# Gate and up of a SwiGLU as a two by two block product with seven multiplications, half of the tokens at a time

## The chip, the cores and the metric

The kernel runs on one core of a Trainium2 chip. The metric is the device time in microseconds (us). The core has a matrix engine (TensorE, PE in the rows), a vector engine (VectorE, DVE), an activation engine (ScalarE, ACT), a general engine (GpSimd, POOL), and queues that start transfers; weights stream from DRAM, and sums of matmuls build up in PSUM. Each engine takes its own instructions in their order.

## What is computed

The reference is one layer of a decoder on 1032 tokens (1024 of a prompt, 8 samples), with D = 1024 features and an inner width of 2816 in both feed-forward parts:

```
def swiglu(x, wg, wu, wd):
    return (silu(x @ wg) * (x @ wu)) @ wd

h = x + 1/2 * swiglu(rms(x), wg1, wu1, wd1)      # first feed-forward part
z = rms(h) @ w_in                                # input projection
h = h + concat(rms(attention(z)), headrms(mlstm(z))) @ w_out
h = h + 1/2 * swiglu(rms(h), wg2, wu2, wd2)      # second feed-forward part
y = rms(h + sigmoid(rms(h) @ w_ple_gate) * (p @ w_ple_proj))
```

All of it is float32. The kernel splits each float32 operand into a rounded part `hi` and a rest `lo`, and makes each product of two tiles from three matmuls (hi hi, hi lo, lo hi).

## The kernel before

Features lie on the partitions, tokens along the free axis. The tokens are cut in G = 3 groups of N = 344. `loadw` loads a weight tile and `split` makes its two parts: a cast on ScalarE (L178) and a subtraction on VectorE (L182), on GpSimd where it is told so (L180).

In a feed-forward part (`ffn`) a unit is one tile of 128 inner features and one token group: `mmg` makes 24 matmuls of 128x344 for gate into PSUM tile `pg`, 24 for up into `pu` (L196 to L198), then ScalarE takes silu, VectorE multiplies (L353) and splits the product into `hdh` and `hdl`. Each of the 22 inner tiles has its gate and up weights loaded and split once, for all three groups. After a block of inner tiles (`FBLOCKS` = 5, 5, 5, 5, 2) the down product follows: for each of 8 output tiles and each group one PSUM tile `pd`, added to the residual stream `h` by VectorE (L365).

At the start (`begin`) the first part multiplies x by the norm's gain alone (`lift`, L293) and leaves each token's scale to what follows the products (L347, L349), so that TensorE starts before the sums of squares are known. Elsewhere the norms of the next part (`norm_a`, `norm_b`; L249 to L279) are made group by group, while TensorE still works on the other groups: in the last block of an `ffn` (`halves`, `close`), and in the input projection behind it.

The order on each engine is that of the program text as `Emitter` hands it out; tiles in SBUF come from one ring (`big`, 43 tiles), PSUM has 8 tiles.

## Time and profile before

| | us |
|---|---|
| median of 3 runs | 2420.05 |
| lowest, highest run | 2419.57, 2423.83 |
| span of the profiled execution | 2381.1 |
| around the span (median less span) | 38.95 |
| TensorE busy | 2294.8 |
| VectorE busy | 1084.0 |
| ScalarE busy | 732.8 |
| GpSimd busy | 416.5 |

The span runs from the first to the last instruction of the profiled execution. A run's time is longer than that by what lies ahead of the first and behind the last instruction. A matmul's duration in the rows reaches from its entry to the end of its result, and matmuls overlap; what one costs in a stream is the distance from one start to the next.

### The profile page before, as it was taken

Reading aid. Unit: us, or ns where it says so; the run is one execution under the profiler, and the core shown is the slowest. Engines: PE = TensorE matmul, PEld = TensorE weight load, DVE = VectorE, ACT = ScalarE, POOL = GpSimd, SP = SyncE. Lnnn points to the kernel's source line nnn. Section 1 sums busy time; section 2 is a strip of 40 time slices with the busy share of each in tenths; the row PEclk is TensorE's granted clock in tenths of the full one; section 3 lists DMA queues with packets and bytes.
Section 4 is the critical chain, followed back from the end, with each engine's and each line's share of the span. In section 5 each row is a group of like instructions: output and inputs, shape, how many; then the busy total and the mean of one; then the engine's idle time right before and its main releaser. Section 6 shows DMA issues by size and latency. Waiting matters only on the chain.

```text
span 2381.1 us, 35330 instructions
## 1 busy us (share of the span) xinstructions
PE 2294.8 (96%) x14479; PEld 2220.7 (93%) x14479; DVE 1084.0 (46%) x2231; ACT 732.8 (31%) x1496; POOL 416.5 (17%) x403
## 2 busy tenths in 40 slices
PE   8999999999998999999888889999999999999997
PEld 7999999999998999999666679999999999999996
DVE  7332332333335656447766677623223223223575
ACT  5211211202213334444655553411121120211353
POOL 4101101101103321102565314200000000000233
PEclk9999999999999999999989989999999999999998
DMA  3111011120121313224964530111111112112213
GB/s 134 38 52 60 29 55 54 32 75 28 43 75 59 109 48 93 82 86 165 260 164 134 160 136 28 45 38 52 55 33 54 56 32 70 33 38 78 62 38 107
DMA packets 77883, 177.84 MB, mean 75 GB/s; under 512 B 11200, under 2 KB 37408, under 8 KB 77720
## 3 DMA queue, kind: packets, MB, share of 16 engines
q1 hardware_dynamic: 67432, 153.22, 21.1%
q0 software_dynamic: 6832, 18.12, 2.9%
q10 hardware_dynamic: 3456, 4.23, 0.6%
q8 instruction: 114, 1.87, 0.3%
q14 instruction: 49, 0.40, 0.1%
HBM read 146.58 MB, written 28.95 MB: 74 GB/s over the span
## 4 chain that ended last, share of the span: by engine, by line
PE 82%; DVE 9%; DMA 4%; ACT 3%; issue 2%; POOL 1%; SPq 0%; ACTq 0%; DVEq 0%; POOLq 0%
PE pd L197 7%; PE pd L198 7%; PE pd L196 7%; PE pg L198 7%; PE pu L197 7%; PE pu L196 7%; PE pu L198 7%; PE pg L197 7%; PE pg L196 7%; PE pz L197 3%; PE pz L196 3%; PE pz L198 3%; DVE xf L279 2%; PE po L1211 1%; DMA kt<-in_cT,idx_t 1%
## 5 line engine op out<-in xcount | busy, mean ns | idle before, releaser
L196 PE MATMUL pd<-hdh,wh 128*128 128x344 f32 x1056 | 341.0, 323 | 5.8 <-ACT hdh L178 5.8
L197 PE MATMUL pd<-hdl,wh 128*128 128x344 f32 x1056 | 340.0, 322 | 3.4 <-DVE hdl L182 3.3
L197 PE MATMUL pg<-xn,wh 128*128 128x344 f32 x1056 | 338.6, 321 | 4.5 <-DVE xn L182 3.8
L198 PE MATMUL pd<-hdh,wl 128*128 128x344 f32 x1056 | 339.7, 322 | 0.0
L196 PE MATMUL pg<-xn,wh 128*128 128x344 f32 x1056 | 338.1, 320 | 0.9 <-ACT xn L178 0.9
L196 PE MATMUL pu<-xn,wh 128*128 128x344 f32 x1056 | 338.5, 321 | 0.3 <-DVE si L347 0.3
L198 PE MATMUL pu<-xn,wl 128*128 128x344 f32 x1056 | 337.8, 320 | 0.8 <-DVE wl L182 0.8
L198 PE MATMUL pg<-xn,wl 128*128 128x344 f32 x1056 | 337.9, 320 | 0.5 <-DVE wl L182 0.3
L197 PE MATMUL pu<-xn,wh 128*128 128x344 f32 x1056 | 337.9, 320 | 0.0
L178 ACT CAST wh<-wr 128x1024 fp32r<-128x1024 f32 (+2 forms) x195 | 180.4, 935 | 371.8 <-PE pd L197 291.2
L182 DVE TENSOR_TENSOR wl<-wr,wh 128x1024 fp32r<-128x1024 f32 (+2 forms) x195 | 215.5, 1105 | 116.3 <-ACT wh L178 111.5
L353 DVE TENSOR_TENSOR hp<-si,pu 128x344 f32<-128x344 f32 x132 | 67.7, 513 | 420.5 <-PE pu L198 413.0
L365 DVE SCALAR_TENSOR_TENSOR h<-pd,h 128x344 f32<-128x344 f32 x240 | 123.2, 515 | 280.1 <-PE pd L198 280.1
L254 POOL TENSOR_TENSOR sq<-sq,sq 128x344 f32<-128x344 f32 x66 | 70.6, 1070 | 798.6 <-ACT sq L249 770.7
L196 PEld LDWEIGHTS pd<-hdh,wh 128*128 128x128 f32 x1056 | 200.0, 189 | 7.1 <-ACT hdh L178 6.7
L197 PEld LDWEIGHTS pg<-xn,wh 128*128 128x128 f32 x1056 | 198.7, 188 | 6.4 <-DVE xn L182 5.2
L197 PEld LDWEIGHTS pd<-hdl,wh 128*128 128x128 f32 x1056 | 200.0, 189 | 4.6 <-DVE hdl L182 4.2
L198 PEld LDWEIGHTS pd<-hdh,wl 128*128 128x128 f32 x1056 | 200.0, 189 | 0.0
L196 PEld LDWEIGHTS pg<-xn,wh 128*128 128x128 f32 x1056 | 198.6, 188 | 1.5 <-ACT xn L178 1.2
L198 PEld LDWEIGHTS pg<-xn,wl 128*128 128x128 f32 x1056 | 198.7, 188 | 1.1 <-DVE wl L182 1.1
L198 PEld LDWEIGHTS pu<-xn,wl 128*128 128x128 f32 x1056 | 198.6, 188 | 1.1 <-DVE wl L182 1.1
L196 PEld LDWEIGHTS pu<-xn,wh 128*128 128x128 f32 x1056 | 198.6, 188 | 1.0 <-issue 0.8
(384 smaller groups left out, 4174.9 us busy)
## 6 DMA issues: line engine op xcount, KB each, us to landing
wr<-in_wu SPq DMA_DIRECT2D x44, 512.0 KB, 3.6
wr<-in_wg SPq DMA_DIRECT2D x43, 512.0 KB, 3.7
wr<-in_wd SPq DMA_DIRECT2D x64, 320.0 KB, 2.9
wr<-in_w_in SPq DMA_DIRECT2D x22, 512.0 KB, 3.8
h<-in_xT SPq DMA_DIRECT2D x24, 172.0 KB, 4.2
hsp<-h SPq DMA_DIRECT2D x8, 516.0 KB, 3.4
ppd<-pj SPq DMA_DIRECT2D x24, 172.0 KB, 2.2
h<-hsp SPq DMA_DIRECT2D x8, 516.0 KB, 5.9
```

What stands on the lines that cost most here:

```text
L178: act.copy(hi, src)
L182: dve.tensor_tensor(out=lo, in0=src, in1=hi.bitcast(F32), op=ALU.subtract)
L196: pe.matmul(ps, whi, xhi, start=first, stop=False)
L197: pe.matmul(ps, whi, xlo, start=False, stop=False)
L198: pe.matmul(ps, wlo, xhi, start=False, stop=last)
L254: pool.tensor_tensor(out=acc[0], in0=acc[0], in1=q, op=ALU.add)
L279: dve.scalar_tensor_tensor(out=x, in0=s[:, c], scalar=gc[:, g0 + k:g0 + k + 1], in1=r, op0=ALU.mult, op1=ALU.mult)
L353: dve.tensor_tensor(out=p, in0=s, in1=pu, op=ALU.mult)
L365: dve.scalar_tensor_tensor(out=h[m][:, c], in0=pd, scalar=0.5, in1=h[m][:, c], op0=ALU.mult, op1=ALU.add)
L1211: pe.matmul(po[:, j0 * 128:512], vtok[kb][:, hd, :], px[:, i, j0:4, :].rearrange("p j q -> p (j q)"), start=(kb == 0 and i == 0), stop=(kb ...
```

## The change

The tokens are cut in four quarters of 258 instead of three groups of 344, in the whole kernel. A feed-forward part goes through all its 22 inner tiles for one half of the tokens (two quarters), then through all of them again for the other half. Gate and up are taken as chains: a chain is two inner tiles, one of the two matrices, one half of the tokens. Its weights are four blocks (two inner tiles by two halves of the 1024 features, a11 to a22), its tokens four blocks (two halves of the features by two quarters), and the product of the two by two blocks is made from seven block products of 4 x 3 matmuls of 128x258, 84 in all, where eight would be the plain way. There are 22 chains per half.

The token operands `b11, b21, t2, t1, t3, t4, b22` are made once per half in `operands` (16 multiplications of 128x258, four differences of 128x1032, seven splits of 128x1032). The weight operands are made per chain in `weights`: three splits of 128x1024, one of 128x512, two sums of 128x512 on GpSimd and two on VectorE. As the weights are used by one half and then by the other, they are loaded, combined and split twice. The results are put together from PSUM: ScalarE copies three partial sums per chain (c1, u2, u3), VectorE adds three. The down products (blocks of 4 and at last 2 inner tiles) are put between the block products (`pump`). The norm of the first half is made before the chains begin (there is no `lift`), that of the second half at the end of the first half's chains. `h` is kept as two halves, one of which goes to DRAM and back.

```diff
-G = 3
+G = 4
 N = T // G
...
-FBLOCKS = [5, 5, 5, 5, 2]
+PBLOCKS = [2, 2, 2, 2, 2, 1]
+NP = NF // 2
+NCH = 2 * NP
+HC = T // 2
+HALF = ((0, 1), (2, 3))
...
+    NAMES = ("b11", "b21", "t2", "t1", "t3", "t4", "b22")
+
+    def operands(h, hf, rs, g0, x):
+        def put(n, src):
+            hi, lo = B([128, 4, N], F32R, "xh"), B([128, 4, N], F32R, "xl")
+            split(hi, lo, src)
+            x[n] = (hi, lo)
...
+        b11 = block(0, 0)
+        put("b11", b11)
+        yield
+        b21 = block(1, 0)
+        put("b21", b21)
+        yield
+        b12 = block(0, 1)
+        t1 = comb(b12, b11)
+        b11 = None
+        b22 = block(1, 1)
+        t2 = comb(b22, t1)
+        put("t2", t2)
+        yield
+        put("t1", t1)
...
+        comb(b22, b12, b12)
+        put("t3", b12)
...
+        comb(b21, t2, b21)
+        put("t4", b21)
...
+        put("b22", b22)
+
+    def weights(ap, j):
+        r1, r2 = (B([128, 2, 512], F32, "wr") for _ in range(2))
...
+            put(("b11", "b21"), r1)
+            s1 = B([128, 512], F32, "ws")
+            pool.tensor_tensor(out=s1, in0=a21, in1=a22, op=ALU.add)
+            pool.tensor_tensor(out=a21, in0=a11, in1=a21, op=ALU.subtract)
+            dve.tensor_tensor(out=a11, in0=s1, in1=a11, op=ALU.subtract)
+            yield
+            dve.tensor_tensor(out=a12, in0=a12, in1=a11, op=ALU.subtract)
+            put(("t2", "b22"), r1)
+            yield
+            hl = B([128, 2, 512], F32R, "wa")
+            split(hl[:, 0], hl[:, 1], s1)
+            o["t1"] = (hl[:, 0], hl[:, 1])
+            yield
+            put(("t3", "t4"), r2)
...
+        def start(i):
+            c = st[i] = {"b1": PS([128, N], "c1"), "b2": PS([128, N], "c2"), "b3": None}
...
+            product(c["b1"], i, "b11", True)
+            c["c1"] = SC(p="c1")
+            act.copy(c["c1"], c["b1"])
+            product(c["b2"], i, "b21", True)
+            dve.tensor_tensor(out=c["o"][:, 0], in0=c["b2"], in1=c["c1"], op=ALU.add)
...
+        def u2(i):
+            c = st[i]
+            product(c["b1"], i, "t2", False)
+            c["u2"] = SC(p="u2")
+            act.copy(c["u2"], c["b1"])
+            c["b3"] = PS([128, N], "c3")
+            product(c["b3"], i, "t1", True)
...
+        ready(0)
+        want(1)
+        for i in range(NCH):
+            start(i)
+            if i:
+                c21(i - 1)
+            want(i + 2)
+            ready(i + 1, 1)
+            u2(i)
+            ready(i + 1, 1)
+            if i:
+                c12(i - 1)
+            ready(i + 1, 1)
+            u3(i)
+            ready(i + 1)
+            after_chain(i)
...
+        ffn_half(h, 0, x, wg, wu, wd, pre, chain_a, tail_a)
+        drain(box["g"])
+        after(0)
+        ffn_half(h, 1, x2, wg, wu, wd, pre2, lambda i: last(i - NCH), last)
+        after(1)
```

In the rows that follow a name's number tells tiles apart; `xf` and `xt` are token blocks, `xl` and `wl` the rests of split token and weight operands.

VectorE at the program's start, before: from its third instruction on it lifts the slices of x as they land and splits the first weight tile behind two of them.

```order
L293 TENSOR_SCALAR xf_131<-h_79,gc 128x344
L293 TENSOR_SCALAR xf_135<-h_80,gc 128x344
L182 TENSOR_TENSOR xn_93<-xf_135,xn_92 128x344
L182 TENSOR_TENSOR wl_141<-wr_139,wh_140 128x512 x2
L293 TENSOR_SCALAR xf_154<-h_81,gc 128x344
L293 TENSOR_SCALAR xf_158<-h_82,gc 128x344
L293 TENSOR_SCALAR xf_162<-h_83,gc 128x344
L293 TENSOR_SCALAR xf_166<-h_84,gc 128x344
```

After: the last of its rows ahead of, and up to, the first chain's weights (`wl_245` is the rest of `b11, b21`; 27 rows for sums of squares, norms and blocks stand ahead of these).

```order
L334 SCALAR_TENSOR_TENSOR xf_215<-h_115,gc,rk_148 128x258 x2
L339 TENSOR_TENSOR xt_220<-xf_215,xt_213 128x1032
L339 TENSOR_TENSOR xf_208<-xf_215,xf_208 128x1032
L339 TENSOR_TENSOR xf_199<-xf_199,xt_220 128x1032
L183 TENSOR_TENSOR xl_223<-xt_220,xh_222 128x1032
L183 TENSOR_TENSOR xl_227<-xt_213,xh_226 128x1032
L183 TENSOR_TENSOR xl_232<-xf_208,xh_231 128x1032
L183 TENSOR_TENSOR xl_237<-xf_199,xh_236 128x1032
L183 TENSOR_TENSOR xl_241<-xf_215,xh_240 128x1032
L183 TENSOR_TENSOR wl_245<-wr_120,wh_244 128x1024
L389 TENSOR_TENSOR wr_120<-ws_248,wr_120 128x512
L391 TENSOR_TENSOR wr_120<-wr_120 128x512
```

The first weight rest moved from the fourth of these rows, ahead of most of the tokens, to a place behind all of the token operands.

VectorE in the middle of the first feed-forward part, before, where a block's down products are added to the residual and the next weights are split:

```order
L365 SCALAR_TENSOR_TENSOR h_79<-pd_4086,h_79 128x344
L365 SCALAR_TENSOR_TENSOR h_79<-pd_4103,h_79 128x344
L365 SCALAR_TENSOR_TENSOR h_79<-pd_4120,h_79 128x344
L182 TENSOR_TENSOR wl_4310<-wr_4308,wh_4309 128x640
L365 SCALAR_TENSOR_TENSOR h_80<-pd_4143,h_80 128x344
L365 SCALAR_TENSOR_TENSOR h_80<-pd_4160,h_80 128x344
L365 SCALAR_TENSOR_TENSOR h_80<-pd_4177,h_80 128x344
L182 TENSOR_TENSOR wl_4367<-wr_4365,wh_4366 128x640
L365 SCALAR_TENSOR_TENSOR h_81<-pd_4200,h_81 128x344
L365 SCALAR_TENSOR_TENSOR h_81<-pd_4217,h_81 128x344
```

After, at the change from the first to the second half of the tokens (`xl_4388` to `xl_4450` and `xt` are operands of the second half, `pd_4477` a down product of the first, `wl_4412` the rest of the weights of the first half's last eight down products):

```order
L466 SCALAR_TENSOR_TENSOR h_113<-pd_4477,h_113 128x258
L466 SCALAR_TENSOR_TENSOR h_113<-pd_4485,h_113 128x258
L339 TENSOR_TENSOR xt_4378<-xf_4373,xf_4327 128x1032
L334 SCALAR_TENSOR_TENSOR xf_4380<-h_3714,gc,rk_3928 128x258 x2
L334 SCALAR_TENSOR_TENSOR xf_4380<-h_3715,gc,rk_3928 128x258 x2
L339 TENSOR_TENSOR xt_4385<-xf_4380,xt_4378 128x1032
L339 TENSOR_TENSOR xf_4373<-xf_4380,xf_4373 128x1032
L339 TENSOR_TENSOR xf_4350<-xf_4350,xt_4385 128x1032
L183 TENSOR_TENSOR xl_4388<-xt_4385,xh_4387 128x1032
L183 TENSOR_TENSOR xl_4406<-xt_4378,xh_4405 128x1032
L183 TENSOR_TENSOR wl_4412<-wr_4409,wh_4411 128x1024
L183 TENSOR_TENSOR xl_4425<-xf_4373,xh_4424 128x1032
```

The weights of the last down products came to stand behind the operands of the second half.

VectorE in the middle of the units, before: scale of a unit's gate, product with up, splits.

```order
L347 TENSOR_TENSOR si_3262<-pg_3212,qz 128x344
L182 TENSOR_TENSOR wl_3330<-wr_3328,wh_3329 128x1024
L353 TENSOR_TENSOR hp_3266<-si_3262,pu_3213 128x344
L182 TENSOR_TENSOR wl_3336<-wr_3334,wh_3335 128x1024
L182 TENSOR_TENSOR hdl_3153<-hp_3266,hdh_3152 128x344
L347 TENSOR_TENSOR si_3320<-pg_3270,qz 128x344
L353 TENSOR_TENSOR hp_3324<-si_3320,pu_3271 128x344
L182 TENSOR_TENSOR hdl_3153<-hp_3324,hdh_3152 128x344
```

After, in the middle of the chains (`wr_1869` and `ws_2076` are weight blocks being combined, `wl_2129` and `wl_2179` rests of weight operands, `hp` and `gs` results):

```order
L389 TENSOR_TENSOR wr_1869<-ws_2076,wr_1869 128x512
L527 TENSOR_TENSOR hp_1993<-c_317_2094,u_326_2175 128x258
L391 TENSOR_TENSOR wr_1869<-wr_1869 128x512
L543 TENSOR_TENSOR hp_1993<-hp_1993,gs_1799 128x258
L466 SCALAR_TENSOR_TENSOR h_114<-pd_2197,h_114 128x258
L183 TENSOR_TENSOR wl_2110<-wr_2107,wh_2109 128x1024
L511 TENSOR_TENSOR hp_1993<-c_302_1991,gs_1799 128x258
L183 TENSOR_TENSOR wl_2129<-wr_1869,wh_2128 128x1024
L466 SCALAR_TENSOR_TENSOR h_114<-pd_2239,h_114 128x258
L183 TENSOR_TENSOR wa_2160<-ws_2076,wa_2160 128x512
L183 TENSOR_TENSOR wl_2179<-wr_1870,wh_2178 128x1024
L500 TENSOR_TENSOR gs_2184<-c_330_2183,c_333_2211 128x258
```

Where before one or two whole weight splits stood between the rows that read PSUM, there are now two sums and four splits per chain (`wl_2110` belongs to a down product).

## Rows read from the trace of the kernel before

**Rows 1.** The page: span, busy time of each engine, shares of the chain that ended last.
```profile
span 2381.1 us, 35330 instructions
...
PE 2294.8 (96%) x14479; PEld 2220.7 (93%) x14479; DVE 1084.0 (46%) x2231; ACT 732.8 (31%) x1496; POOL 416.5 (17%) x403
...
PE 82%; DVE 9%; DMA 4%; ACT 3%; issue 2%; POOL 1%; SPq 0%; ACTq 0%; DVEq 0%; POOLq 0%
```

**Rows 2.** Windows (start:end, length; busy us and instructions per engine; clock, DMA, GB/s).
```profile
0.00:20.00 20.00, 16.13 (x87) 14.52 (x88) 15.22 (x29) 11.81 (x26) 8.06 (x12) 1.00 0.91 315
20.00:150.00 130.00, 124.54 (x775) 121.58 (x775) 64.39 (x102) 43.26 (x79) 31.15 (x30) 1.00 0.13 41
150.00:300.00 150.00, 150.00 (x954) 150.00 (x953) 45.66 (x75) 26.18 (x43) 14.28 (x14) 1.00 0.15 47
...
750.00:800.00 50.00, 41.89 (x243) 40.05 (x243) 43.62 (x66) 23.04 (x45) 22.52 (x20) 0.93 0.40 142
...
2220.00:2300.00 80.00, 75.47 (x456) 73.18 (x455) 58.10 (x87) 40.66 (x75) 30.17 (x27) 0.98 0.19 56
```

**Rows 3.** Timeline of TensorE: the warming-up (start, duration in us, count).
```profile
1.07 5.56 PE L443 MATMUL pw<-ones 128*128 128x128 f32 x28 [1.07 <-DVE epsc L426]
```

**Rows 4.** Matmul groups by form (count, busy us, mean ns, idle time before).
```profile
L196 PE MATMUL pd<-hdh,wh 128*128 128x344 f32 x1056 | 341.0, 323 | 5.8 <-ACT hdh L178 5.8
...
L197 PE MATMUL pg<-xn,wh 128*128 128x344 f32 x1056 | 338.6, 321 | 4.5 <-DVE xn L182 3.8 <-POOL xn L180 0.8
...
L197 PE MATMUL pj<-pel,wj 128*128 128x344 f32 x48 | 16.9, 351 | 0.0
```

**Rows 5.** Timeline of TensorE: 256 columns, then 512.
```profile
1156.22 0.28 PE L1164 MATMUL pss<-kTh,qTh 96*128 96x256 f32 x1
1156.34 0.28 PE L1165 MATMUL pss<-kTl,qTh 96*128 96x256 f32 x1
1156.45 0.28 PE L1166 MATMUL pss<-kTh,qTl 96*128 96x256 f32 x1
1156.57 0.39 PE L196 MATMUL ps<-uvh,ckh 128*128 128x512 f32 x1
1156.80 0.40 PE L197 MATMUL ps<-uvh,ckh 128*128 128x512 f32 x1
```

**Rows 6.** Timeline of TensorE: sixteen matmuls of one column and the next one.
```profile
943.26 1.84 PE L806 MATMUL pb<-sq,ct 128*128 128x1 f32 x16
944.96 0.40 PE L196 MATMUL pz<-u,wh 128*128 128x344 f32 x1
```

**Rows 7.** VectorE groups by form, whole span.
```profile
L182 DVE TENSOR_TENSOR wl<-wr,wh 128x1024 fp32r<-128x1024 f32 x129 | 160.4, 1244 | 79.9 <-ACT wh L178 79.7
L365 DVE SCALAR_TENSOR_TENSOR h<-pd,h 128x344 f32<-128x344 f32 x240 | 123.2, 515 | 280.1 <-PE pd L198 280.1
...
L182 DVE TENSOR_TENSOR PT<-pT,PT 128x512 fp32r<-128x512 f32 x48 | 32.2, 684 | 6.0 <-ACT PT L178 5.6
...
L279 DVE SCALAR_TENSOR_TENSOR z<-z,gc,r 128x344 f32<-128x344 f32 x15 | 7.7, 570 | 0.0
```

**Rows 8.** ScalarE groups by form, whole span.
```profile
L178 ACT CAST wh<-wr 128x1024 fp32r<-128x1024 f32 x129 | 132.7, 1043 | 128.7 <-PE pd L197 111.3 <-DMA wr<-in_wd 5.4 <-DMA wr<-in_wu 4.9
...
L267 ACT ACT_TABLE_LOAD x10 | 12.8, 1283 | 31.7 <-PE ns L263 31.6
```

**Rows 9.** Timelines: one VectorE operation twice, and GpSimd beside the second.
```profile
763.10 0.52 DVE L182 TENSOR_TENSOR hdl<-hp,hdh 128x344 fp32r<-128x344 f32 x1
...
768.21 1.22 DVE L182 TENSOR_TENSOR hdl<-hp,hdh 128x344 fp32r<-128x344 f32 x1
...
766.00 4.20 POOL L254 TENSOR_TENSOR sq<-sq,sq 128x344 f32<-128x344 f32 x4
```

**Rows 10.** GpSimd groups by form, whole span.
```profile
L349 POOL TENSOR_TENSOR si<-si,mask_qk 128x344 f32<-128x344 f32 x22 | 20.4, 926 | 364.2 <-ACT si L348 364.2
...
L799 POOL TENSOR_TENSOR vb<-vb,kws 128x1024 f32<-128x1024 f32 x4 | 7.6, 1899 | 65.4 <-DMA vb<-vsd 42.6 <-DVE nst L796 22.7
```

More of the change, by code (lines that the diff above doesn't have):

```diff
@@ L426, in trunk @@
     dve.memset(epsc, EPS)
[L427 to L433 removed]
+    h = Rows()
     warm = C([128, 1], name="warm")
@@ L484, in consts, with ffn, chain_a, tail_a @@
             sp.dma_start(out=t, in_=I[n])
[L485 to L489 removed]
+        dve.memset(qzr, 0.0)
+    def ffn(g0, wg, wu, wd, first_rows, first_scales, next_rows, after, last, x=None):
+        pre = ({}, {}, {})
+        if x is None:
+            x = {}
+            first_rows()
+            pre[0][0] = weights(wg, 0)
+            drain(operands(h, 0, first_scales(), g0, x))
+        box = {}
+        def chain_a(i):
+            if i == NCH - 3:
+                next_rows()
+            if i == NCH - 2:
+                box["s"] = [stat(h, g) for g in HALF[1]]
+            if i == NCH - 1:
+                box["r"] = [s() for s in box.pop("s")]
+        pre2 = ({}, {}, {})
+        x2 = {}
+        def tail_a(n):
+            if n == 0:
+                pre2[0][0] = weights(wg, 0)
+                box["g"] = operands(h, 1, box.pop("r"), g0, x2)
+            next(box["g"], None)
+        ffn_half(h, 0, x, wg, wu, wd, pre, chain_a, tail_a)
[3 more added lines that the diff above has]
+        after(1)
@@ new lines, in rows_x, with scales_x, following, apply @@
+    def rows_x():
+        act.activation(warm, epsc, RSQ)
+        pw = PS([128, 128], "pw")
+        for i in range(WARM):
+            pe.matmul(pw, ones, ones, start=i == 0, stop=i == WARM - 1)
+        sp.dma_start(out=gc, in_=I["gcols"])
+        h.load(I["xT"], 0)
+    def scales_x():
+        fs = [stat(h, g) for g in HALF[0]]
+        return [f() for f in fs]
+    def following(x, g0, keep, ahead):
+        scales = {}
+        def apply(g):
+            x.alloc(g)
+            scaled(scales[g // 2][g % 2], h.srcs(g), x.outs(g), g0)
+        def after(hf):
+            box = []
+            def sums():
+                box.extend(stat(h, g) for g in HALF[hf])
+            def rest():
+                scales[hf] = [f() for f in box]
+                if hf == 0:
+                    h.spill(hsp, 0)
+                else:
+                    apply(2)
+                    apply(3)
+                    if not keep:
+                        h.spill(hsp, 1)
+            if hf == 0:
+                em.later(3.0, sums)
+                em.later(9.0, rest)
+            else:
+                sums()
+                em.later(5.0, rest)
+        def last(n):
+            if n == -2:
+                h.load(hsp, 0)
+            if n == 1:
+                apply(0)
+            if n == 6:
+                apply(1)
+                if not keep:
+                    h.t[0] = None
+                ahead()
+        return after, last
```

521 lines of the change are left out of this document (278 added, 243 removed).

## The prediction

> **What bounds the kernel now.** The first look is at the page [rows 1]: TensorE is busy for 2294.8 of 2381.1 us, and 82% of the chain that ended last is TensorE's; VectorE is busy for 46%. So the kernel is bound by its stream of matmuls, and an edit counts by the matmuls that it takes out and by the holes that it puts in. Next come windows, since a share over the whole span hides where the holes are [rows 2]. From 150 to 300 us, in the units of the first feed-forward part, TensorE never stops: 954 matmuls in 150 us, or 157.2 ns for one of 128x344. By that price the other windows show their holes. From 0 to 150 us there are 862 instructions, 28 of them the warming-up [rows 3], so 834 matmuls of 157.2 ns = 131.1 us, and 18.9 us are lost at the start. From 750 to 800 us (end of the first part, start of the input projection) 243 x 157.2 ns = 38.2 us, so 11.8 us are lost. From 2220 to 2300 us (end of the second part) 456 x 157.2 ns = 71.7 us, so 8.3 us are lost. VectorE works 45.66 us of the 150, 30%: inside the units it has room.
>
> **The sum's base.** The profiled execution has a span of 2381.1 us. The median is 2420.05, so 38.95 us lie around the span; I leave these as they are and add the span's change to the median.
>
> **Term 1, the seven products.** There are 6 groups of 1056 gate and up matmuls, 6336 [rows 4]; by 157.2 ns they cost 996 us. After the change there are 4 halves (two parts, two halves each) x 22 chains x 84 = 7392 of 128x258. The trace has none of 258 columns. The nearest rows are three of 256 columns: starts 1156.22, .34, .45 and 1156.57, so 0.35 / 3 = 117 ns; the 512 behind them takes 0.23 us [rows 5]. So the price is proportional to the columns: 117 x 258/256 = 117.9, and 157.2 x 258/344 = 117.9. A floor lies close below: sixteen matmuls of one column take 1.70 us, 106 ns each [rows 6], which is the weight load alone. I take 117.9: 7392 x 117.9 = 871.5 us, a gain of **124.5 us**. All other matmuls of 344 (down to the 3 x 48 of `pj`, 6264 in all [rows 4]) become 4/3 as many at 3/4 of the price: 8352 x 117.9 = 984.7 = 6264 x 157.2, nothing. That zero and the gain hang on the same price: a nanosecond more for each of the 15744 is 16 us. Bounds: 117 ns (-14 us) and 122 ns, if the small excess of [rows 5] were larger in this stream (+64 us).
>
> A rule of the Trainium skill speaks against this term. TensorE: Matmul & The Clock Gate, section Back-to-back issue gap, says that a stream of weight load and matmul pairs is spaced by both, and gives about 81 ns at 128 columns and 131 ns at 512, which is mostly a fixed cost; on that line 258 columns would cost about 0.9 of 344 instead of 0.75 (an estimate from that page). Then 7392 x 0.9 is 6650 against 6336, and the change would lose in its main term and in all the rest. Here [rows 2, 5] give 117, 157.2 and 230, which is a line through nearly zero; the measurement decides, and what is left of the rule is rival 3.
>
> **Term 2, the start.** Before, the first matmul needs one lifted slice and half a weight tile. After, VectorE has 37 rows up to `wl_245`, without which the first product is not complete. Their prices: a subtraction of 128x1024 takes 1.24 us, of 128x512 0.68, a sum of 344 from PSUM 0.515, a scalar_tensor_tensor of 344 from SBUF 0.57 [rows 7]; on the line through these, 258 columns cost 0.41 (0.48 for the last kind). Six sums and eight steps of the norm at 0.41, sixteen multiplications at 0.48, eleven differences and splits of 1032 and one of 1024 at 1.24: 5.7 + 7.7 + 14.9 = 28.3 us. Half of x is 2.1 MB, at 315 GB/s [rows 2] 6.7 us, landed at about 9; behind it the squares end, and the norm's ScalarE step with its table load of 1.28 us [rows 8] stands in the chain, so the norm's steps begin at about 13.5 us, with some 26 us of VectorE to come. The first product starts at about 39.5 us. The combined weights behind it (5.8 us of VectorE against two products of 1.4 us) hold it for one or two us more, and TensorE comes in cold. I take 41 us lost instead of 18.9: **+22 us** (16 to 27).
>
> **Term 3, the middle of each part, new and twice.** When the first half's last chain ends with its product b22, TensorE has 4 down products of 12 and 8 of 6 matmuls left that it can do, 96 x 117.9 ns = 11.3 us, then 8 that need `wl_4412`. VectorE has, from the sum behind b22 to `wl_4412`: 16 multiplications (7.7), nine differences and splits of 1024 or 1032 (11.2), three rows of 516 (2.1), 13 of 258 from PSUM (0.41, as the 0.515 of 344 [rows 7]; 5.3): 26.3 us. TensorE waits 15 us. The 48 matmuls then last 5.7 us, as long as VectorE's next rows, but the combined weights of the next chain (two sums, three splits) come a few us late: 3 us. Coming out of such a hole has a price too: around the 4.8 us of waits in the window of 750 to 800 us the granted clock is 0.93 [rows 2], 3.5 us of 50 lost; as part of that is in the waits I take 2. Together 20 us each, **+40 us** (28 to 54). What is late there is nothing but VectorE's queue; ScalarE's casts (1.04 us [rows 8]) run ahead of it.
>
> **Term 4, the other ends.** At the end of the first part, the quarters of the first half have their norm done long before, and eight units of the input projection (22.6 us) can run while the last two quarters' norm is made: the 11.8 us mostly vanish, **-10**. At the end of the second part the per-layer weights' splits stand behind the norm's rows: 18.5 us of VectorE, some 2.5 us of latencies, less 5.9 us of matmuls in hand, so 16 to 18 us instead of 8.3: **+9**. The second part's first operands are made beside the last twelve units of the output projection (34 us of TensorE, 40 of VectorE); before, the norms there cost some waits too: 0, from -5 to +6.
>
> **Term 5, inside the chains.** A half has 22 x 84 + 1056 down matmuls, 2904 x 117.9 ns = 342.4 us. VectorE has for it 88 splits of 1024 (109 us), 88 rows of 512 or 516 (22 splits, 44 sums, 22 splits of results: 60), 33 rows of multiplications (17), 66 PSUM sums (27), 96 down sums (40), and operands and norms (32): 285 us, 83% where it was 30%. Beside that, GpSimd's 44 sums block it: a row of 344 takes VectorE 0.52 us, and 1.22 while GpSimd runs [rows 9]. A GpSimd sum of 512 costs about 1.17 us (0.93 for 344, 1.90 for 1024 [rows 10]), so up to 51 us: 336 of 342. TensorE uses weights a whole chain (15.6 us) after VectorE may begin them, and in the rows of the order three or four rows stand between a sum and the split of it, longer than ScalarE's cast in between. So TensorE stays the bound, with some stalls where rows bunch: 0.1 us per chain, 88 chains, **+8** (0 to 80). The second load of all weights is hidden: before, windows of units move 47 GB/s and the start 315 [rows 2].
>
> **Sum.** -124.5 + 22 + 40 - 10 + 9 + 8 = -55.5 us; 2420.05 - 55.5 = **2364.5 us**.
>
> **Rivals.** (1) VectorE becomes the bound inside the chains, the case on the other side. If the blocked 51 us come whole, and the 22 casts between a sum and its split are waited for as well (1.24 us each, 27), VectorE needs 363 of 342 us per half: +21 us, four times, +84 in place of +8: 2440. It decides from the point where waits add 57 us to the 285 of a half. For it: [rows 9], and that each engine keeps its order. Against it: GpSimd's sums need nothing but landed weights, and the rows between. The Trainium skill (SBUF — State Buffer, section SBUF: two separate sides) calls the pair of ports that GpSimd and VectorE share an exclusive lock held for a whole instruction; the 0.52 and 1.22 us of [rows 9] agree. Chance 0.13. (2) Smaller stalls, half a us per chain, from ScalarE's copies of PSUM waiting behind casts: +44 in place of +8, 2400. For it: a partial sum must be copied within two products, 2.8 us. Against: ScalarE is about half busy. 0.13. (3) A fixed cost per matmul: at 121 ns all 15744 cost 50 us more, 2414; [rows 5] speak against it. 0.06. (4) The holes of terms 2 and 3 are half as large, because VectorE's rows start earlier than I count: -31, 2333. For: ScalarE and the transfers run ahead. Against: the last sum behind b22 stands in the same queue. 0.13. (5) Matmuls nearer the floor of [rows 6], 112 ns: -93, 2271; 0.03. My forecast (2345 to 2385) has 0.52.
>
> **Range and chances.** Rivals 1 and 5 lie outside, with part of 4: I give 2325 to 2425. Runs of this kernel lie within 0.18% of each other, so 0.2% (4.8 us) is about what can be told from no change. Below 2415: forecast, 2, 4, 5 and part of 3, 0.83; within 0.2%: 0.04; above: rival 1, 0.13.
>
> **What would show it.** Steps in the new profile: windows inside the chains with 118 ns per matmul (150 us: 1272); the first product at 38 to 42 us; two holes of 15 to 20 us near a quarter and three quarters of the feed-forward time, waiting for VectorE's split of down weights; at the end of the second part a wait for a weight split; VectorE's share near 80% in the chains. Wrong would be waits of c1, u2 or weights in every chain (rivals 1, 2), or starts 121 ns apart in windows without waits (3).

## The result, and the profile after

The changed kernel takes 2521.15 us (median of 4 runs, 2518.75 to 2523.04), the kernel before 2419.81 us beside it (4 runs, 2413.15 to 2423.83). The ratio is 1.0417, with an interval of 1.0399 to 1.0435: slower by about 101 us, where 55 us less had been forecast.

The page of the changed kernel, in the lines that answer to [rows 1]: span, busy time of each engine, shares of the chain that ended last, and the line of a GpSimd sum that is new.

```profile
span 2517.5 us, 44055 instructions
...
PE 2256.6 (90%) x17645; PEld 2170.9 (86%) x17645; DVE 1672.0 (66%) x3154; ACT 1107.6 (44%) x2139; POOL 619.3 (25%) x538
...
PE 72%; DVE 15%; ACT 5%; issue 3%; DMA 2%; another core or an unknown queue 1%; POOL 0%; SPq 0%; DVEq 0%; ACTq 0%; POOLq 0%
...
L387 POOL TENSOR_TENSOR ws<-wr 128x512 f32<-128x512 f32 x88 | 148.4, 1687 | 1076.1 <-PE c L431 347.4
```

TensorE's busy time fell by 38 us only, and the span has 261 us in which it is idle instead of 86 (some 39 of the difference lie in the attention; 30 of these 39 are in the kernel before as well when it is profiled again, see below). VectorE took 588 us more. The share of TensorE in the chain that ended last fell from 82% to 72%, that of VectorE rose from 9% to 15%.

Windows of the changed kernel (columns as in [rows 2]): the start, two windows of chains in the first feed-forward part with its middle between them, the end of that part, the start of the second part (with the output projection ahead of it), and the second part's middle.

```profile
0.00:150.00 150.00, 111.37 (x848) 107.61 (x848) 108.62 (x150) 68.10 (x115) 35.80 (x31) 0.86 0.31 102
...
100.00:340.00 240.00, 236.42 (x1957) 235.21 (x1956) 164.66 (x245) 105.36 (x167) 50.56 (x30) 1.00 0.31 102
...
340.00:500.00 160.00, 127.44 (x965) 124.37 (x964) 121.56 (x182) 71.35 (x125) 36.01 (x30) 0.89 0.29 93
500.00:750.00 250.00, 245.15 (x2029) 243.51 (x2028) 170.85 (x256) 110.42 (x173) 50.21 (x30) 1.00 0.30 98
...
750.00:820.00 70.00, 66.91 (x540) 66.23 (x539) 50.37 (x92) 28.75 (x59) 19.54 (x20) 0.98 0.44 146
...
1499.00:1640.00 141.00, 128.27 (x992) 126.06 (x992) 94.61 (x160) 49.96 (x97) 37.32 (x37) 0.94 0.25 87
...
1900.00:2100.00 200.00, 166.15 (x1271) 162.04 (x1270) 147.17 (x219) 87.41 (x149) 45.80 (x36) 0.91 0.31 100
```

To read them as the prediction reads [rows 2], the price of a matmul of 128x258 is needed. The cleanest row for it is one of the experiment `plain8` below, where TensorE never stops for 250 us:

```profile
500.00:750.00 250.00, 250.00 (x2084) 250.00 (x2083) 98.16 (x147) 60.25 (x86) 0.00 (x0) 1.00 0.29 90
```

250 / 2084 = 120.0 ns, where 117.9 had been taken. A window less its matmuls at that price is what was lost in it: 52 us in the first 150 (28 warm-ups and four matmuls of the norm taken off; before 18.9), 5.2 and 6.5 us in the windows of chains, 44.2 and 47.5 in the two middles, 5.2 at the first part's end.

For the other stages the profile of [rows 1] is no match: its span is 38.95 us shorter than the median of the runs. The kernel before was therefore run again (`b_again`), and its span is 2419.6 us. The kernel before takes 2376 to 2379 us in some turns on the chip and 2420 to 2427 us in others, so each run below is compared with the kernel before of its own turn. Stages are cut at the first matmul of each next part:

| stage, us | before (`b_again`) | after | difference |
|---|---|---|---|
| first feed-forward part | 779.9 | 810.6 | +30.7 |
| input projection, mLSTM | 364.2 | 368.2 | +4.0 |
| attention | 305.6 | 319.8 | +14.2 |
| output projection | 96.7 | 109.1 | +12.4 |
| second feed-forward part | 756.1 | 776.8 | +20.7 |
| per-layer part, end | 117.2 | 133.0 | +15.8 |
| span | 2419.6 | 2517.5 | +97.9 |

Both feed-forward parts, in which 125 us were to be saved, became longer. The windows of the two parts, after and in `b_again`, tell what was saved and what was lost:

```profile
0.00:810.65 810.65, 728.44 (x5849) 718.75 (x5850) 573.27 (x861) 354.32 (x584) 177.70 (x131) 0.95 0.31 100
1607.81:2384.57 776.76, 724.57 (x5817) 715.47 (x5817) 544.99 (x817) 339.28 (x555) 171.30 (x118) 0.97 0.30 100
```
```profile
0.00:779.86 779.86, 766.14 (x4790) 760.23 (x4791) 296.19 (x482) 175.69 (x300) 105.32 (x105) 0.99 0.18 58
1546.33:2302.42 756.09, 753.21 (x4760) 752.09 (x4759) 234.35 (x369) 151.99 (x253) 20.20 (x18) 1.00 0.16 49
```

By 120.0 and 157.2 ns the matmuls of both parts together cost some 101 us less than before. But 109 and 79 us are lost in the two parts, where 27 and 8 were: 153 us more.

The waits of TensorE in the first middle, 340 to 470 us (line waited for, us in total, times, longest):

```profile
PE pd L197 <- ACT wh L179: 11.5, 1, 11.5
PE pd L197 <- ACT hd L179: 7.9, 1, 7.9
PE c L429 <- ACT u L518: 4.7, 1, 4.7
PE pd L199 <- DVE wl L183: 1.9, 1, 1.9
```

The first and the last of these are the wait that the prediction had counted (13.4 us, for 15). The others it had not. The timeline of ScalarE shows what stands behind the first:

```profile
410.71 1.06 ACT L179 CAST xh<-xf 128x1032 fp32r<-128x1032 f32 x1 [5.05 <-DVE xf L334]
420.51 2.00 ACT L179 CAST xh<-xt 128x1032 fp32r<-128x1032 f32 x2 [8.73 <-DVE xt L339]
422.42 1.04 ACT L179 CAST wh<-wr 128x1024 fp32r<-128x1024 f32 x1
```

The cast of the down weights needs nothing that is late, but it stands behind casts of the second half's operands, and these wait 8.73 us for VectorE's differences. So ScalarE does not run ahead of VectorE: it hangs on it, in order. In this wait that costs little, as VectorE's split of the same weights ends only at 426.1 us. The wait for `hd` is the same case one step earlier, and there it costs: a weight cast on ScalarE, itself waiting 5.1 us for VectorE's `L391`, stands ahead of the cast of the chain's result. `L391` is late in its turn because GpSimd's weight sums (`L387`, `L388`) and VectorE's (`L389`) stand among sums of squares (`sq`) of the second half's norm. The rows of GpSimd, VectorE and ScalarE:

```profile
361.82 1.45 POOL L388 TENSOR_TENSOR wr<-wr,wr 128x512 f32<-128x512 f32 x1
...
362.08 2.35 DVE L275 TENSOR_TENSOR sq<-sq,sq 128x258 f32<-128x258 f32 x2
364.35 1.21 DVE L389 TENSOR_TENSOR wr<-ws,wr 128x512 f32<-128x512 f32 x1
365.60 1.10 DVE L391 TENSOR_TENSOR wr<-wr 128x512 f32<-128x512 f32 x1
...
366.74 1.04 ACT L179 CAST wh<-wr 128x1024 fp32r<-128x1024 f32 x1 [5.14 <-DVE wr L391]
```

The wait for `u` is one for a copy out of PSUM that stands behind squares of the first half's next norm, that of the input projection:

```profile
442.84 1.03 ACT L179 CAST wh<-wr 128x1024 fp32r<-128x1024 f32 x1
443.77 0.72 ACT L268 ACTIVATE sq<-h 128x258 f32<-128x258 f32 x2
444.40 0.35 ACT L518 COPY u<-c 128x258 f32<-128x258 f32 x1
```

And behind these waits TensorE runs at half of its clock for a while (granted clock 0.50). The windows behind the waits for `hd`, for the down weights, for `u`, and behind one of 2.1 us for a weight split (`wa`) that ended at 479.6 us:

```profile
368.36:373.60 5.24, 4.48 (x19) 4.19 (x20) 3.96 (x6) 2.59 (x4) 0.00 (x0) 0.50 0.47 113
426.19:431.62 5.43, 5.43 (x25) 5.43 (x26) 5.43 (x8) 1.08 (x2) 0.00 (x0) 0.50 0.88 276
445.28:448.69 3.41, 3.41 (x19) 3.41 (x18) 3.20 (x4) 0.38 (x1) 2.74 (x2) 0.50 0.00 0
479.62:482.82 3.20, 3.20 (x15) 3.20 (x16) 1.08 (x1) 0.00 (x0) 0.00 (x0) 0.50 0.00 0
```

TensorE's timeline behind the wait for `u` (starts 0.215 us apart, then 0.12):

```profile
444.80 0.39 PE L429 MATMUL c<-xh,wh 128*128 128x258 f32 x1 [4.67 <-ACT u L518]
445.02 0.28 PE L430 MATMUL c<-xl,wh 128*128 128x258 f32 x1
...
446.75 0.42 PE L430 MATMUL c<-xl,wh 128*128 128x258 f32 x1
446.96 0.42 PE L431 MATMUL c<-xh,wl 128*128 128x258 f32 x1
...
448.68 0.29 PE L430 MATMUL c<-xl,wh 128*128 128x258 f32 x1
448.81 0.28 PE L431 MATMUL c<-xh,wl 128*128 128x258 f32 x1
```

### The profile page after: what moved, and what is told of

It reads as the page before. It is cut to its first block, busy times and chain, and to the rows that moved or that the text cites. A ratio compares the mean times of both kernels' runs of the same rounds, so it can differ in the third digit from the quotient of the medians.

```text
span 2517.5 us, 44055 instructions
## 1 busy us (share of the span) xinstructions
PE 2256.6 (90%) x17645; PEld 2170.9 (86%) x17645; DVE 1672.0 (66%) x3154; ACT 1107.6 (44%) x2139; POOL 619.3 (25%) x538
## 4 chain that ended last, share of the span: by engine, by line
PE 72%; DVE 15%; ACT 5%; issue 3%; DMA 2%; another core or an unknown queue 1%; POOL 0%; SPq 0%; DVEq 0%; ACTq 0%; POOLq 0%
PE c L431 10%; PE c L429 10%; PE c L430 10%; PE pd L198 6%; PE pd L199 6%; PE pd L197 6%; DVE wl L183 4%; PE pz L198 3%; PE pz L197 3%; PE pz L199 3%; ACT wh L179 2%; PE po L1426 1%; PE pl L199 1%; PE pl L198 1%
## 5 line engine op out<-in xcount | busy, mean ns | idle before, releaser
L429 PE MATMUL c<-xh,wh 128*128 128x258 f32 x2112 | 607.1, 287 | 50.2 <-ACT wh L179 40.2
L183 DVE TENSOR_TENSOR wl<-wr,wh 128x1024 fp32r<-128x1024 f32 x390 | 505.3, 1298 | 220.3 <-ACT wh L179 183.1
L431 PE MATMUL c<-xh,wl 128*128 128x258 f32 x2112 | 606.4, 287 | 20.3 <-DVE wl L183 20.2
L430 PE MATMUL c<-xl,wh 128*128 128x258 f32 x2112 | 602.9, 285 | 0.0
L179 ACT CAST wh<-wr 128x1024 fp32r<-128x1024 f32 x390 | 406.0, 1047 | 259.4 <-DMA wr<-in_wd 79.1
L429 PEld LDWEIGHTS c<-xh,wh 128*128 128x128 f32 x2112 | 406.1, 192 | 53.9 <-ACT wh L179 43.2
L197 PE MATMUL pd<-hd,wh 128*128 128x258 f32 x1408 | 403.2, 286 | 44.2 <-ACT wh L179 26.7
L431 PEld LDWEIGHTS c<-xh,wl 128*128 128x128 f32 x2112 | 405.5, 192 | 27.1 <-DVE wl L183 26.7
L387 POOL TENSOR_TENSOR ws<-wr 128x512 f32<-128x512 f32 x88 | 148.4, 1687 | 1076.1 <-PE c L431 347.4
L430 PEld LDWEIGHTS c<-xl,wh 128*128 128x128 f32 x2112 | 407.6, 193 | 0.1
L198 PE MATMUL pd<-hd,wh 128*128 128x258 f32 x1408 | 402.5, 286 | 4.8 <-DVE hd L183 4.8
L197 PEld LDWEIGHTS pd<-hd,wh 128*128 128x128 f32 x1408 | 269.4, 191 | 46.4 <-ACT wh L179 27.6
L198 PEld LDWEIGHTS pd<-hd,wh 128*128 128x128 f32 x1408 | 269.9, 192 | 6.9 <-DVE hd L183 6.9
L388 POOL TENSOR_TENSOR wr<-wr,wr 128x512 f32<-128x512 f32 x88 | 140.1, 1592 | 6.6
```

Source lines behind the costliest of these rows:

```text
L179: act.copy(hi, src)
L183: dve.tensor_tensor(out=lo, in0=src, in1=hi.bitcast(F32), op=ALU.subtract)
L197: pe.matmul(ps, whi, xhi, start=first, stop=False)
L198: pe.matmul(ps, whi, xlo, start=False, stop=False)
L387: pool.tensor_tensor(out=s1, in0=a21, in1=a22, op=ALU.add)
L388: pool.tensor_tensor(out=a21, in0=a11, in1=a21, op=ALU.subtract)
```

## The experiments

What could have lost the time: the second half's operands, which stand ahead of what TensorE needs in the middles; GpSimd's sums of weights, late and in VectorE's way (rival 1's mechanism); the clock behind the holes; or the cutting into halves and quarters itself. All are one profiled run, but for `bestA` and `bestE`. Where the kernel before ran beside them at 2420 to 2427 us, stages and spans are compared with those of after (span 2517.5). Where it ran at 2376.3 or 2379.3 us, the difference to it is given; for after that difference is +101.3 us.

**The kernel before, again (`b_again`).** No edit.

> The kernel before, unchanged, profiled once more. In the shown profiles the attention stretch (first score matmul to first output projection) lasts 266 us before and 320 after, 54 of the 136 us by which the spans differ, while the medians differ by 101 us. Theory: the change itself lengthens that stretch; then it lasts 262 to 272 us here too and the span is near 2381. Rival: the profiled execution of before was a quick one in that stretch; then it lasts 295 to 310 us here and the span is 2410 to 2425.

Measured: 2421.36 us with a span of 2419.6, so 1.8 us lie around the span, and not 38.95. In the first part its rows repeat [rows 2]: 150 to 300 us holds 955 matmuls for 954. The attention differs: 305.6 us for 266.2 in the profile of [rows 1]. The last section has its rows.

**More down products kept for the middle (`hold20`)**, 20 in hand ahead of the first half's last block for `HOLD` = 4:

```diff
-rate[0] = max(0.0, (left + 16 - HOLD) / (nxt - 3.0)) if b + 1 < len(PBLOCKS) else 0.0
+keep = 20 if hf == 0 and b + 2 == len(PBLOCKS) else HOLD
+rate[0] = max(0.0, (left + 16 - keep) / (nxt - 3.0)) if b + 1 < len(PBLOCKS) else 0.0
```

> Changed kernel, but in the first half of each feed-forward part the 16 down products of the last block of four and the four left over are all kept for the change of halves, so that TensorE has 39.7 us of matmuls in hand there instead of 17. Theory (the holes at the change of halves come from VectorE's queue, 26 us of operand work ahead of the last down weights, and cost about 39 us each with the clock's fall behind them): both holes shrink by 13 us of waiting and some 8 of half clock, 2521 falls to 2475 to 2490. Rival (the time is lost by the chains' own stalls, and taking the down products out of the chains ahead of the change makes VectorE late there): no gain or a loss, 2515 to 2535.

Measured: 2509.87 us, span 2508.1, 9.4 us less than after, under a third of what had been expected. The feed-forward parts gain 3.8 and 6.4 us. The wait of 11.5 us is cut into several: from 330 to 500 us there are waits of 9.1 us in two for the down weights and a new one of 6.8 us for chain weights. Work in hand moves the hole; VectorE's queue stays as long.

**The second half takes the first half's operands (`reuse`)**, so that no operands are made in the middle (this leaves out the second half's operands and multiplies the first half's again; only its time counts):

```diff
-if i == NCH - 1:
+if i == NCH - 1 and hf == 1:
     x.pop(n)
...
-box["g"] = operands(h, 1, box.pop("r"), g0, x2)
+x2.update(x)
```

> Changed kernel; the second half of each feed-forward part uses the first half's token operands again, so the operands of the second half are not made at all (its result for the second half of the tokens is another one). Theory: without the 26 us of VectorE work at the change the waits for the last down weights go, and the clock stays up: 35 to 60 us less in all, 2460 to 2485. Rival (the hole is set by the norm's sums and by ScalarE's squares ahead of the copies, not by the operands): at most 15 us less.

Measured: 2476.85 us, span 2475.0, 42.5 us less than after. First part 789.8 us, second 759.8: 20.8 and 17.0 us less than after. The wait for the down weights is gone, that for `hd` (7.9 us) and that for `u` are still there. So the operands are worth about 20 us a part, the size that the prediction had given its hole; the other half of each middle is something else. As these two waits stay, they do not hang on the operands.

**No weight sums on GpSimd (`nopool`)**; a22 stands for the sum, also in the split of it, and a21 stays unsummed, so the products are other ones and only the time counts:

```diff
-pool.tensor_tensor(out=s1, in0=a21, in1=a22, op=ALU.add)
-pool.tensor_tensor(out=a21, in0=a11, in1=a21, op=ALU.subtract)
-dve.tensor_tensor(out=a11, in0=s1, in1=a11, op=ALU.subtract)
+dve.tensor_tensor(out=a11, in0=a22, in1=a11, op=ALU.subtract)
```

> Changed kernel; GpSimd's two weight sums per chain are left out (the other operations take the unsummed blocks, so the products are other ones). Theory (GpSimd blocks VectorE's operations with two SBUF sources, and so makes the stalls inside the chains and part of the holes): matmuls per 50 us inside the chains rise from 411 to 416 or more, VectorE's mean for a 128x1024 split falls from 1298 to 1240 ns, the time by 15 to 30 us. Rival (the stalls come from the order on ScalarE and VectorE alone): the split's mean falls, the matmul rate and the time stay within 8 us.

Measured: 2452.6 us, span 2450.8, 66.7 us less than after, where 15 to 30 had been expected. Its windows:

```profile
100.00:340.00 240.00, 239.16 (x1991) 238.95 (x1990) 158.20 (x247) 101.91 (x162) 0.00 (x0) 1.00 0.30 101
...
340.00:500.00 160.00, 137.96 (x1069) 136.25 (x1068) 122.50 (x197) 78.88 (x137) 14.35 (x16) 0.91 0.32 104
```

The chains lose 240 - 1991 x 0.12 = 1.1 us for 5.2, the middle 31.7 for 44.2. Here two of four sums per chain are gone and with them all waits for GpSimd's weight sums; the two runs that follow part these.

**The sum in a buffer of its own (`wspool`)**, not in the ring (two of the scratch pool's twelve buffers pay for it):

```diff
-s1 = B([128, 512], F32, "ws")
+s1 = wsp.tile([128, 512], F32, tag="ws", name=nm("ws"))
```

> Changed kernel with GpSimd's first weight sum in a buffer of its own (the scratch pool pays with two of twelve), so that GpSimd's sums wait for landed weights and the last use of that one buffer, not for a tile of the full ring that matmuls still read. Theory (leaving the sums out gained 68 us because VectorE stands waiting for sums that start late: 14.5 us of 240 in the chains): those waits go, 2521 falls by 25 to 45 us. Rival (it is the blocking of VectorE while GpSimd runs, whenever it runs): the sums still take as long, the time falls by less than 12 us.

Measured: 2481.33 us, span 2479.5: 38.0 us less than after, for a buffer. In the changed kernel the timelines of GpSimd and VectorE show what it takes away:

```profile
141.18 2.13 POOL L387 TENSOR_TENSOR ws<-wr 128x512 f32<-128x512 f32 x1 [13.31 <-PE c L430]
143.40 1.29 POOL L388 TENSOR_TENSOR wr<-wr,wr 128x512 f32<-128x512 f32 x1
...
144.72 0.69 DVE L389 TENSOR_TENSOR wr<-ws,wr 128x512 f32<-128x512 f32 x1 [1.59 <-POOL wr L388]
```

The sum's weights have landed, but the ring hands it a tile that matmuls still read. When TensorE lets it go GpSimd begins, two sums one behind the other, and VectorE's third sum, in front of all its other work, waits for their end. Over the span that line's idle time, with its own form, is this for after and for `wspool` (its lines are one further):

```profile
L389 DVE TENSOR_TENSOR wr<-ws,wr 128x512 f32<-128x512 f32 x88 | 65.9, 749 | 59.5 <-POOL wr L388 59.2
```
```profile
L390 DVE TENSOR_TENSOR wr<-ws,wr 128x512 f32<-128x512 f32 x88 | 61.3, 697 | 5.4 <-POOL wr L389 2.6
```

59.5 us of VectorE's time became 5.4. The chains now lose 1.0 us of the 240 for 5.2, as little as in `nopool`. And the wait for `hd` ahead of the middle shrinks, as GpSimd's sums for that chain are now done at 342.8 us, ahead of the squares, and not at 363.3:

```profile
340.61 2.15 POOL L389 TENSOR_TENSOR wr<-wr,wr 128x512 f32<-128x512 f32 x1
...
PE pd L198 <- ACT hd L180: 2.5, 1, 2.5
```

**All four sums on VectorE (`dvesum`):**

```diff
-pool.tensor_tensor(out=s1, in0=a21, in1=a22, op=ALU.add)
-pool.tensor_tensor(out=a21, in0=a11, in1=a21, op=ALU.subtract)
+dve.tensor_tensor(out=s1, in0=a21, in1=a22, op=ALU.add)
+dve.tensor_tensor(out=a21, in0=a11, in1=a21, op=ALU.subtract)
```

> Changed kernel with both weight sums on VectorE in place of GpSimd: 176 more VectorE operations of 128x512, 0.69 us each, 121 us more work for it, none for GpSimd in the chains. Theory (GpSimd's lateness and its blocking cost more than the sums themselves): 20 to 45 us faster than the changed kernel. Rival (VectorE's own load is what stalls the chains): each half is 10 us longer or more, 2530 to 2580.

Measured: 2502.76 us, span 2501.0: 16.5 us less than after, though VectorE has 88 x (0.699 + 0.696) = 123 us more to do. That is less than the 20 to 45 us expected, but a gain. What VectorE gets back is the wait of 59.5 us and shorter rows: the split of 128x1024 takes 1.232 us as in `nopool`, for 1.298 beside GpSimd's sums (and 1.369 in `wspool`), 390 times.

**A longer warming-up (`warm`):**

```diff
-WARM = 14
+WARM = 110
```

> Changed kernel with 110 in place of 14 warming-up matmuls at the start, which keep TensorE busy to about the first product. Theory (the clock is at half until 49.3 us and costs there 4 to 5 us): the first feed-forward part is 4 to 7 us shorter, and nothing else changes. Rival (the products behind the first wait for weights anyway): at most 2 us.

Measured: 2527.76 us, span 2525.8, 8.3 us more than after: inconclusive. The warm-ups end at 28.5 us, the norm's matmuls stand behind them in TensorE's order, and the first product moves from 40.06 to 51.93 us. TensorE is idle ahead of it for 22.4 us again, as in the changed kernel, and its first matmuls are slow again. The clock at the start was not separated from the wait by this.

**Eight products (`plain8`)**, everything else as in the changed kernel (halves, quarters, weights loaded and split twice); no sums of operands or weights, 96 matmuls per chain for 84:

```diff
-put(("b11", "b21"), r1)
-s1 = B([128, 512], F32, "ws")
...
+put(("a11", "a12"), r1)
+yield
+put(("a21", "a22"), r2)
...
+for k in range(2):
+    product(ps, i, wa[k], xb[k], k == 0, tq == 1, wt == 1)
```

> Changed kernel with its quarters, halves, double weight loads and down products, but gate and up as eight plain block products: no sums of blocks, no copies of partial sums, four token operands and four weight blocks. Theory (the seven products save what they cost in matmuls, some 125 us, and what they bring on VectorE, GpSimd and ScalarE takes most of that back): TensorE has 1056 matmuls of 119 ns more, 126 us, and the stalls inside chains and two thirds of the holes go, 70 to 90 us: 2555 to 2580. Rival (halves and quarters are what costs, the sums are hidden): 2620 to 2650.

Measured: 2501.39 us, +125.1 (before 2376.3). Its feed-forward parts take 819.8 and 788.3 us: 40 and 32 more than before, 9 and 11.5 more than after. So the cutting costs 72 us in these two stages before a product is saved (27 of them are the price: 12672 matmuls at 120.0 ns for 9504 at 157.2), and of the 4 x 22 x 12 = 1056 matmuls that are saved, 127 us at 120.0 ns, only 21 remain there. The chains of `plain8` lose nothing (the row above), its middle 160 - 1159 x 0.12 = 20.9 us:

```profile
340.00:500.00 160.00, 146.37 (x1159) 145.22 (x1159) 81.34 (x136) 54.67 (x92) 15.06 (x16) 0.95 0.31 102
```

**Weights of the last part ordered earlier (`look8`):**

```diff
-LOOK = 3
+LOOK = 8
```

> Changed kernel with all eight weight tiles of the per-layer gate asked for ahead (8 in place of 3 looked ahead), so that six of the eight splits stand ahead of the last norm's rows on VectorE. Theory (the 16 us hole at the end of the second part is a wait for a weight split behind the norm's rows): the last stage is 118 to 123 us long instead of 133, all else as it was. Rival (the norm itself is late): the hole stays and changes its releaser, 130 us or more.

Measured: 2504.7 us, span 2502.7, 14.8 us less than after. The last stage takes 123.2 us for 133.0: TensorE's wait of 16.3 us for the cast of the per-layer weights is now one of 5.7 us in two, for their splits. Term 4's reason for that wait was right.

**Cures together.** `wh20` is `wspool` with `hold20`; `wh12l` is `wspool`, 12 products in hand, and the squares of the first half's later norm put off:

```diff
-em.later(3.0, sums)
-em.later(9.0, rest)
+em.later(10.0, lambda: box.append(stat(h, HALF[0][0])))
+em.later(18.0, lambda: box.append(stat(h, HALF[0][1])))
+em.later(26.0, rest)
```

> GpSimd's sum in its own buffer, and 20 down products kept for the change of halves. Theory (the two losses lie in different places, sums in the chains, operands at the change): the gains add up, 40 and 11 or more: 2460 to 2475. Rival (both are VectorE's lateness, and one cure does for both): 2476 to 2490.

> As the run before, with 12 down products kept, and the 32 squares of the following norm put off from behind the change of halves to later in the second half's first chain, quarter by quarter. Theory (partial sums' copies wait behind the squares on ScalarE, 5 us per change): 5 to 10 us less than with GpSimd's buffer and 20 kept. Rival (something else is late there): the same within 4 us.

Measured: 2421.85 us (+45.5) and 2411.93 us (+35.6). The feed-forward parts of `wh20` are together 51 us shorter than those of after, where `wspool` alone gives 45 and `hold20` 10, so these two nearly add up; those of `wh12l` are 62 us shorter. The middle of `wh12l`:

```profile
340.00:500.00 160.00, 141.99 (x1118) 139.80 (x1117) 134.73 (x202) 78.62 (x138) 47.49 (x34) 0.94 0.33 112
```

25.8 us are lost in it for 44.2, most of it in one wait of 9.5 us for the down weights and one of 3.9 us for a copy. VectorE is busy for 134.73 of the 160 us. A version of the changed kernel that also spread the second half's sums of squares over two chains (`spread`) came to a deadlock and has no time, so what the squares ahead of `hd` cost by themselves is not shown.

`bestC` is `wh12l` with 16 in hand and the last down weights cast ahead of the last products; `bestA` adds to that the per-layer weights earlier and a part's first weights between its operands (below); `bestE` is `wh12l` with `look8` and those first weights:

```diff
+raw = weights(wg, 0)
+og = operands(h, 0, first_scales(), g0, x)
+wk = raw()
+pre = ({}, {0: next(wk)}, {0: wk})
+for q in (og, wk, og, og, wk, og, wk, og, wk):
+    next(q, None)
```

> The same without the last two cures (per-layer weights, first chain's weights). Theory: the feed-forward parts' middles as there; the last stage about 135 us as in the changed kernel instead of 118 to 122, the first product at 37.5 us and not before 30.

> All cures together: GpSimd's sum in its own buffer, 16 down products kept for the change of halves with their weights split ahead of the operands, the squares put off, four per-layer weights split ahead of the last norm, and the first chain's weights of each part split beside the operands. Theory (each hole is a place in an engine's queue, and nothing else holds the seven products back): per part 10 to 15 us less than with GpSimd's buffer, 12 down products kept and late squares, the start of the second part 6 to 10 less, the last stage 15 less; the stage from the first projection's start to the attention and the attention itself stay as they are in the changed kernel. Against the kernel before on the same chip 0.985 to 0.998. Rival (VectorE's load per half is what lasts): the holes only move, 1.005 to 1.015.

> GpSimd's sum in its own buffer, 12 down products kept, squares put off, first chain's weights beside the operands, all per-layer weights ahead. Theory (gains add up where they lie in different stages): against the earlier set without the last two cures the stage before the second part is 6 us shorter, the last stage 12 to 16, the two parts the same within 5: 2385 to 2395 on a chip where before takes 2379, a ratio of 1.002 to 1.008. Rival (VectorE's sum of work near the changes is the bound, cures move holes): the ratio is 1.012 or more.

Measured: `bestC` 2432.9 us (+53.6); `bestA` 2416.22 for 2379.28 before (5 runs), ratio 1.0166, interval 1.0145 to 1.0188; `bestE` 2433.06 for 2421.49 (6 runs), ratio 1.005, interval 1.0032 to 1.0068. The output projection's stage fell from 109.1 to 101.8 us with the first weights between the operands, in both. In `bestE` the first part takes 780.0 us and the second 739.4, for 779.9 and 756.1 before. Not all cures helped. `bestC` spans 21.0 us more than `wh12l`, with parts of 789.7 and 753.1 us for 782.5 and 743.3; which of its two additions costs this was not parted. `bestA`, for which 0.985 to 0.998 had been expected, has the same additions, and its wait for the per-layer weights is still 17.3 us: ordering their loads earlier did not help there, while `look8`'s edit did. In `bestE` the first product comes at 21.06 us for 40.06, but 46 us are lost in the first 150 for 52 in after and 49 in `wspool`: the earlier first product by itself gained little. No version beats the kernel before.

## Why the prediction was wrong

By its own steps; "lost" is worked out as above, and the base is `b_again` where a stage is compared.

| step | predicted, us | measured, us |
|---|---|---|
| Term 1, matmuls | -124.5 | 7392 x 0.1200 - 996 = -109; the others 8352 x 0.1200 - 984.7 = +17.5; -91.5 |
| Term 2, start | +22 | 52 lost in 150 us for 18.9: +33 |
| Term 3, two middles | +40 | 44.2 + 47.5 = +92 |
| Term 4, first part's end | -10 | 5.2 for 11.8: -7 |
| Term 4, second part's first operands | 0 | 141 - 992 x 0.12 = 22 lost, 2.6 before: +19 |
| Term 4, second part's end | +9 | last stage +15.8 |
| Term 5, chains | +8 | 5.2 + 6.5 in 490 us of the first part: some +25 in both parts, an estimate by doubling |
| attention | none | +14 |
| sum | -55.5 | +100 |

The rows are of windows and of stages that meet at their edges, and the one of the chains is doubled; that their sum comes near the measured 97.9 us is in part luck.

**The step that failed most is Term 3, "together 20 us each"**, and in it the sentence that nothing is late there but VectorE's queue, as ScalarE's casts run ahead of it. What it counted came true: VectorE's rows from the sum behind b22 (400.51) to the split of the down weights (426.0) took 25.5 us for 26.3, and TensorE waited 13.4 us for 15. But ScalarE, in order, stood behind a cast that waited for VectorE's weight sums, and behind squares of a norm, and so gave two more waits, for `hd` and `u`, 12.6 us; small ones follow. Neither those sums nor the squares stand in Term 3's count. The clock was counted with 2 us: after four of the waits TensorE worked at half of its clock for 3.2 to 5.4 us, some 17 us in all, of which by 215 and 120 ns some 7 us are lost. `reuse` gives 20 us a part for the operands, `nopool` 12.5 for what GpSimd adds in the first middle.

**Term 5's reason failed too: GpSimd's sums needed more than landed weights.** They needed a tile of the ring. That is the fact which rival 1 had against it, and which `wspool` refutes with 38 us by one buffer. Rival 1 itself is not what happened: VectorE is busy for 164.66 of 240 us in the chains, 69% where 83% to 98% had been worked out, and the loss there is a few us in a hundred. It lies in waits of at most 1.0 us, most of them for weight splits. Nor is it rival 2: all waits of products for copies of `u` (`L518`) in the span are 9.4 us, the two of 4.7 us in the middles. GpSimd's sum took 1.69 us where 1.17 had been estimated from [rows 10], and lengthened VectorE's splits, whose mean in `nopool` (1.232) is near that of [rows 7]. That this is paid in the middles and at the ends, which VectorE fills, is argued and not shown: in `wspool` the splits are longer still (1.369), and it is 38 us faster. The page of the Trainium skill that the prediction named for rival 1 (SBUF — State Buffer, section SBUF: two separate sides) puts an exclusive lock between these two engines. The trace agrees in its direction: the mean split of 128x1024 is 1.298 us with GpSimd's sums and 1.232 without.

**Term 1 was right in kind and mis-sized by 33 us.** The matmul of 128x258 costs 120.0 ns, between the 117.9 taken and the 121 of rival 3. The 117 ns came from three starts of 256 columns, printed to 0.01 us [rows 5]; on a price that 15744 matmuls pay, that was too few. The two streams of this case, 157.2 ns at 344 and 120.0 at 258, lie on a line with 8 ns that do not depend on the columns. The ratio is 0.763, for 0.75 by columns alone. By the rule of the Trainium skill that the prediction weighed (TensorE: Matmul & The Clock Gate, section Back-to-back issue gap) it would be 0.9, an estimate from that page's two figures; the measurement decides, and it stays far nearer to the columns.

**Term 2** had the first product at 39.5 us (it came at 40.06), and then 1 to 2 us of waits. The longest of these was 2.5 us, and up to 100 us they are 5.7 us in all; behind the longest the timeline shows starts 0.215 us apart from 43.7 to 49 us (granted clock 0.50), which costs again as much as that wait. VectorE has 42 rows up to `wl_245`, as many as the term priced; the 37 that it names, and the 27 that are said to stand ahead of the listed ones (31 do), are slips that change no sum.

**Term 4** had the second part's first operands hidden, by 34 us of TensorE beside 40 of VectorE. They were hidden; the weights of the first chain, split behind them, were not, and TensorE waited 9.6 us for them. `bestA` and `bestE` take 7.3 us out by putting them between. At the end of that part 16.3 us of waiting came as predicted (16 to 18); of the 15.8 us of that stage, `look8` gives back 9.8.

What `bestE` leaves, beside `b_again`: the two feed-forward parts are together 16.6 us shorter, and the other stages give that back: attention +11.4, per-layer part +5.9, output projection +5.1, input projection and mLSTM +3.5. That VectorE's work is the limit of further cures is argued from its 134.73 us of 160 in the middle of `wh12l`, and not shown by a run of its own. Why the attention grew by 14.2 us (by 6.4 where it is short, 272.6 in `wh20` for 266.2) was not tried.

## What to carry to other kernels

Saving matmuls by sums of operands moves work to the engines that make the operands; what counts is not their mean share but the place where the operands of a whole stage are due at once, and there an in-order engine that "only casts" can be as late as the engine it casts for. Measure the price of the new matmul shape in a stream of hundreds before multiplying it by thousands, and add to the waits what the clock behind them costs: here some 7 us for 28 us of waits in a middle, and 2.5 us for one of 2.5 us at the start. Give short-lived results that a helper engine makes a buffer of their own: in a ring they can wait for the slowest reader of the tile before, as here for matmuls.

## What the runs showed of the hardware

A wait of TensorE of 2.1 us (ended at 479.6 us) was followed by 3.2 us at half of the clock, and one of 4.67 us by 3.4. Behind the one of 4.67 us two matmuls still started 0.12 us apart (445.02 to 445.26 us), and the half clock came only then. The same program had two lengths of its attention stretch: 266 to 274 us in all kernels of some turns on the chip, 305 to 322 in all kernels of others. In the short form TensorE's longest waits there are for transfers and VectorE; in the long one the trace gives part of the time to nothing that it can name, as here in `b_again`, 1100 to 1480 us:

```profile
PE pss L1164 <- issue: 13.8, 4, 11.9
PE pT L1196 <- DVE PT L182: 6.9, 2, 6.0
```

What differs between these turns is open; nothing in the kernels does. It is why the profile of [rows 1] is 38.95 us shorter than the runs beside it, which the prediction had put around the span: `b_again` has 1.8 us around its span, and an attention 39.4 us longer.
